# Merge gates computed first, in seven-product form and token-major, in a one-core hybrid decoder layer

## The chip, the cores and the metric

The kernel runs on one core of one Trainium2 chip. Its time is device microseconds of that core; the number given for a kernel is the median of its runs. The kernel before took 1704.99 us (three runs: 1705.82, 1704.99 and 1703.16). The rows below come from one profiled execution, whose span from the first to the last instruction is 1703.4 us.

## The reference

One decoder layer on 512 tokens of width 2048, all in float32:

```
h = rmsnorm(x) * norm_gain                      # 512 x 2048
u = h @ w_in                                    # 2048 x 12488 columns:
#   4 x 1024 fox q,k,v,z | 8 forget logits | 4 x 1024 rwkv r,k,v,z | 2 x 96 low rank | 2048 g_a | 2048 g_b
o_a = fox_attention(q, k, v, log_sigmoid(f + bias)) * silu(z_a)     # 8 heads of 128, causal softmax
o_b = (group_norm(rwkv7_scan(r, decay, k, v, kk, kk * a)) + bonus) * silu(z_b)   # 16 heads of 64
m = sigmoid(g_a) * (o_a @ w_proj_fox) + sigmoid(g_b) * (o_b @ w_proj_rwkv)       # 1024 x 2048 each
out = final_rmsnorm(x + m @ w_out)              # 2048 x 2048
```

The four thousand columns `g_a` and `g_b` are the merge gates. The RWKV inputs are shifted by a token before use (`u + (previous u - u) * mu`), and the scan is done in chunks of 64 tokens.

## The kernel before, in words

Every large product is made exact enough by splitting both operands into two parts of TensorE's float32 format, `hi + lo`, and adding three products (hi·hi, hi·lo, lo·hi). So the 128 columns of one tile of `u`, over 16 chunks of the width, are 48 matmuls with 512 moving columns each (the tokens), with the weights stationary. `load_raw` (L237) brings a piece of weights, `split_pieces` makes `whi` on ACT (L262) and `wlo` on DVE (L263); loads run five pieces ahead and splits two. `mm` (L133) and `tr` (L137) are the helpers through which nearly all TensorE instructions go.

The stages, in order:

1. Startup. `norm_rows` (L197 to L211) takes the row norms of x; `turn` (L213 to L225) turns x on TensorE, two chunks of 256 tokens at a time, and writes `hhi` on ACT (L222) and `hlo` on DVE (L225). The tile `u_wd` (low-rank inputs and forget logits) is computed behind the turning, half of the tokens after the other half.
2. `u_ad`, the second low-rank tile.
3. Sixteen units in the order rw0, rw1, fox0, rw2, fox1, ... fox5, rw7, fox6: a pair of RWKV heads (tiles k, r, z, v) or a FoX head (tiles fq, fk, fv, fz).
4. The gates `u_g` (32 tiles), three tiles ahead of the projections `p` that they gate; unit fox7 stands after the third gate tile. A projection tile is 24 matmuls.
5. The output product `o` (765 matmuls and a few more), the residual and the final norm.

The order on TensorE is the order in which the program emits it. The stream of large products is the filler; a worker for each RWKV pair (`rwkv_prep` then `rwkv_chain`) and each FoX head (`fox_head`) puts small products between. A worker yields a distance on an emission clock (the table `LAG`) and is resumed when that much other work was emitted. `until` forces workers on without filler where the stream needs something that a worker has not yet released: unit fox i waits for head i-1 to be emitted to its end, the tile k of pair i for the first step of the preparation of pair i-1. ACT, DVE and POOL are ordered by a scheduler with priorities after `start.close()`.

The scan's chain has eight chunks a pair. Each is `z` on TensorE, its copy `zt` (L689, DVE), `sa` (TensorE), two copies into `SV` (L701 on DVE, L702 on ACT), `st` (TensorE) and the new state (L710, DVE), one after the other. The inverses of the chunk triangles are 31 steps of a multiply (L478) and a sum (L620) on DVE.

Of the kernel before, what the change touches and what calls it, by code (L numbers as in the profile page):

```python
# [9 lines left out]
F32 = mybir.dt.float32  # L10
# [16 lines left out]
FW = 1024  # L27
RW0 = 4 * FW + NH             # first column of the RWKV part of w_in
# [8 lines left out]
# rows of the parameter tile, which is transposed to one column per row  # L37
# [17 lines left out]
def hybrid_layer(  # L55
# [15 lines left out]
    wpool = ctx.enter_context(tc.tile_pool(name="wpool", bufs=1))  # L71
    psm = ctx.enter_context(tc.tile_pool(name="psm", bufs=1, space=PSUM))
# [78 lines left out]
    # ---------------------------------------------------------------- loads and constants
# [4 lines left out]
    xload = ExitStack()  # L156
    xpool = xload.enter_context(tc.tile_pool(name="xpool", bufs=1))
# [4 lines left out]
    junk = xpool.tile([P, D], F32, name="junk")  # L162
# [3 lines left out]
    xts = [xpool.tile([P, D], F32, tag="xt", bufs=4, name=f"x_{tb}") for tb in range(4)]  # L166
# [24 lines left out]
    # ---------------------------------------------------------------- h = rmsnorm(x), transposed, in two parts  # L191
# [40 lines left out]
    used = [0]  # L232

    def load_raw(name, srcs, nk, M):
        raw = wpool.tile([P, nk, M], F32, tag="raw", bufs=RAWS, name=f"raw_{name}")
        for off, src in srcs:
            nc.sync.dma_start(raw[:, :, off:off + src.shape[1]], src.rearrange("(k p) m -> p k m", p=P))  # L237
        return raw

    def next_piece():  # L240
        """The two parts of the next piece of the weights. Loads run ahead of the products by
        RAWS pieces, the splits by two."""
        i = used[0]
# [8 lines left out]
    def split_pieces(n):  # L252
        while len(parts) < min(n, len(pieces)):
# [775 lines left out]
```

## Time and profile before

| | |
|---|---|
| runs | 1703.16 to 1705.82 us, median 1704.99 us |
| profiled execution, span | 1703.4 us |
| TensorE busy | 1669.6 us (98%), 8874 matmuls |
| VectorE (DVE) busy | 958.7 us (56%) |
| ScalarE (ACT) busy | 699.5 us (41%) |
| GpSimd (POOL) busy | 66.5 us (4%) |
| DMA | 170.28 MB, mean 100 GB/s |

The profiled execution is given by its span alone; the median of the runs stands 1.6 us above it. PE is TensorE, PEld its weight loads, DVE VectorE, ACT ScalarE, POOL GpSimd, SP SyncE, whose queue issues most DMAs. A busy time is the time in which an engine had an instruction running. Matmuls are pipelined, so one is listed longer (0.39 us) than the pitch from one to the next.

### The profile page before, as it was taken

To read this page: it belongs to the slowest core of one execution; us is meant where nothing else is said; L and a number is where in the kernel's file an instruction comes from. 1 tells how busy PE (TensorE), PEld (TensorE's weight loads), DVE (VectorE), ACT (ScalarE), POOL (GpSimd) and SP (SyncE) were. 2 spreads that over 40 slices of the span, in tenths; PEclk is the share of its full clock that TensorE was granted. 3 is DMA by queue.
4 is the path that set the end of the run, shared out by engine and by line. 5 is a ranking of instruction groups with operands and counts; after the bars stand their busy time and mean duration, and the time that the engine had idled before them with its cause. 6 is when DMAs were issued, how large, how long until landed. Compare 5 with 4: busy or idle time off the path is not lost.

```text
span 1703.4 us, 24080 instructions
## 1 busy us (share of the span) xinstructions
PE 1669.6 (98%) x8874; PEld 1317.2 (77%) x8874; DVE 958.7 (56%) x2005; ACT 699.5 (41%) x1391; POOL 66.5 (4%) x133
## 2 busy tenths in 40 slices
PE   6999999999999999999999999999999999999998
PEld 5778768677687786877867777888888888888886
DVE  6647568786796677866976645232224333353432
ACT  7532552554445535544454444222223222243322
POOL 3000000000000000000000000000000000001110
PEclk9999999999999999999999999999999999999999
DMA  6334234233233332333334325335334333343422
GB/s 176 77 90 110 68 88 107 61 108 92 69 97 83 86 96 81 102 79 91 82 82 111 88 76 142 98 94 148 94 99 143 98 95 98 96 141 136 136 81 99
DMA packets 287980, 170.28 MB, mean 100 GB/s; under 512 B 38790, under 2 KB 270830, under 8 KB 287222
## 3 DMA queue, kind: packets, MB, share of 16 engines
q1 hardware_dynamic: 284358, 156.13, 33.8%
q0 software_dynamic: 2064, 9.46, 1.6%
q10 hardware_dynamic: 1440, 3.15, 0.5%
q8 instruction: 69, 1.13, 0.3%
q14 instruction: 49, 0.40, 0.1%
HBM read 158.19 MB, written 10.50 MB: 99 GB/s over the span
## 4 chain that ended last, share of the span: by engine, by line
PE 94%; DVE 4%; DMA 1%; SPq 1%; ACT 1%; issue 0%; DVEq 0%; ACTq 0%
PE u_g L133 21%; PE o L133 10%; PE p L133 10%; PE u_fz L133 5%; PE u_fv L133 5%; PE u_fq L133 5%; PE u_r L133 5%; PE u_fk L133 5%; PE u_k L133 5%; PE u_v L133 5%; PE u_z L133 5%; DVE BK L478 2%; PE y L133 1%; PE fo L133 1%; PE sc L133 1%; PE sa L133 1%
## 5 line engine op out<-in xcount | busy, mean ns | idle before, releaser
L133 PE MATMUL u_g<-hhi,whi_g 128*128 128x512 f32 x512 | 200.2, 391 | 0.0
L133 PE MATMUL u_g<-hhi,wlo_g 128*128 128x512 f32 x512 | 200.1, 391 | 0.0
L133 PE MATMUL u_g<-hlo,whi_g 128*128 128x512 f32 x512 | 199.4, 390 | 0.0
L263 DVE TENSOR_TENSOR wlo_g<-raw_g,whi_g 128x512 fp32r<-128x512 f32 x128 | 88.2, 689 | 164.1 <-ACT whi_g L262 159.9
L262 ACT ACTIVATE whi_g<-raw_g 128x512 fp32r<-128x512 f32 x128 | 80.9, 632 | 226.1 <-PE u_g L133 120.1
L133 PEld LDWEIGHTS u_g<-hhi,wlo_g 128*128 128x128 f32 x512 | 96.1, 188 | 20.6
L133 PEld LDWEIGHTS u_g<-hlo,whi_g 128*128 128x128 f32 x512 | 96.1, 188 | 20.3
L133 PEld LDWEIGHTS u_g<-hhi,whi_g 128*128 128x128 f32 x512 | 96.1, 188 | 19.9
L478 DVE TENSOR_TENSOR Wt<-W,Lt 128x16 f32<-128x16 f32 (+30 forms) x248 | 101.7, 410 | 5.4
L133 PE MATMUL p<-ohi,whi_p 128*128 128x512 f32 x256 | 101.2, 395 | 0.5 <-ACT ohi L868 0.5
L263 DVE TENSOR_TENSOR wlo_p<-raw_p,whi_p 128x512 fp32r<-128x512 f32 x64 | 44.3, 692 | 102.0 <-ACT whi_p L262 102.0
L133 PE MATMUL p<-ohi,wlo_p 128*128 128x512 f32 x256 | 100.5, 392 | 0.0
L133 PE MATMUL p<-olo,whi_p 128*128 128x512 f32 x256 | 99.9, 390 | 0.5 <-DVE olo L870 0.5
L262 ACT ACTIVATE whi_p<-raw_p 128x512 fp32r<-128x512 f32 x64 | 40.4, 631 | 122.2 <-PE u_g L133 120.6
L133 PE MATMUL o<-whi_o,mhi 128*128 128x512 f32 x224 | 87.3, 390 | 0.1
L133 PE MATMUL o<-wlo_o,mhi 128*128 128x512 f32 x224 | 87.2, 389 | 0.0
L133 PE MATMUL o<-whi_o,mlo 128*128 128x512 f32 x224 | 87.1, 389 | 0.0
L263 DVE TENSOR_TENSOR wlo_o<-raw_o,whi_o 128x512 fp32r<-128x512 f32 x56 | 41.7, 755 | 63.6 <-ACT whi_o L262 63.4
L620 DVE TENSOR_REDUCE W<-Wt 128x8 f32<-128x16 f32 (+30 forms) x248 | 72.9, 294 | 5.4
L262 ACT ACTIVATE whi_o<-raw_o 128x512 fp32r<-128x512 f32 x56 | 34.7, 629 | 70.0 <-PE o L133 65.8
L133 PEld LDWEIGHTS p<-olo,whi_p 128*128 128x128 f32 x256 | 48.1, 188 | 11.9 <-DVE olo L870 1.1
L695 ACT ACTIVATE pre<-SV,E 64x64 f32<-64x64 f32 x112 | 38.5, 343 | 45.3 <-DVE SV L710 44.0
(352 smaller groups left out, 3892.1 us busy)
## 6 DMA issues: line engine op xcount, KB each, us to landing
raw_g<-in_w_in_dram SPq DMA_DIRECT2D x128, 256.0 KB
raw_o<-in_w_out_dram SPq DMA_DIRECT2D x56, 256.0 KB
raw_k<-in_w_in_dram SPq DMA_DIRECT2D x32, 256.0 KB
raw_r<-in_w_in_dram SPq DMA_DIRECT2D x32, 256.0 KB
raw_z<-in_w_in_dram SPq DMA_DIRECT2D x32, 256.0 KB
raw_v<-in_w_in_dram SPq DMA_DIRECT2D x32, 256.0 KB
raw_fq<-in_w_in_dram SPq DMA_DIRECT2D x32, 256.0 KB
raw_fk<-in_w_in_dram SPq DMA_DIRECT2D x32, 256.0 KB
```

Of the source, the lines that this page charges most:

```text
L133: PE.matmul(out, lhsT=lhsT, rhs=rhs, start=start, stop=stop, **kw)
L262: S.activation(whi, raw, AF.Copy)
L263: (G if j < 4 else V).tensor_tensor(wlo, raw, whi.bitcast(F32), ALU.subtract)
L478: eng.tensor_tensor(o, a, b, op)
L620: V.tensor_reduce(W[:, :, i], tmp[:, :, 0:i + 1], AX.X, ALU.add)
L695: S.activation(pre[hs[q]], SV[q][hs[q], c, :], AF.Copy, scale=E1[hs[q], c, CH:CH + 1])
```

## The change

Five parts, which come together:

1. The gates are computed first, right after `u_ad`, by a new function `fast`. It is the seven-product form of a two-by-two block product (Strassen's, in Winograd's ordering): the tokens are cut in two halves, the width in two halves, and the columns of a group in two blocks of 512. Four groups of 28 units of 12 matmuls make the 4096 columns. Now 128 tokens are stationary and 512 weight columns move.
2. The form needs four sums of blocks of h (`make_sums`, L260 to L273, in the second half of the startup: per step four additions or subtractions and four splits on DVE, four copies on ACT) and four sums of blocks of weights (subtractions of 128 x 1024 on DVE in `prep`). `turn` therefore keeps h in float32 and makes `hhi` with a second ACT copy.
3. The gates go through tanh and are stored in DRAM (`sg_d`, 16 stores of 512 KB on POOL's queue); the merge loads them back tile by tile.
4. The projections are token-major (merged output as stationary, weights moving, 768 matmuls as before), and the merged result is turned back by 64 TensorE transposes (`turn_merged`) before the output product.
5. `UNITS` replaces the alternation at its end by ... fox4, rw6, rw7, fox5, fox6, fox7. The constant `dynamic_dma_scratch_size=4096` is set.

```diff
-units = [("rw", 0), ("rw", 1)]
-for i in range(2, 8):
-    units += [("fox", i - 2), ("rw", i)]
-units += [("fox", 6)]
+UNITS = [("rw", 0), ("rw", 1), ("fox", 0), ("rw", 2), ("fox", 1), ("rw", 3), ("fox", 2), ("rw", 4), ("fox", 3),
+         ("rw", 5), ("fox", 4), ("rw", 6), ("rw", 7), ("fox", 5), ("fox", 6), ("fox", 7)]
...
 def turn(hf, j, dst):
...
-            S.activation(hhi[:, j + i, t], pt[:, i * 256:(i + 1) * 256], AF.Copy, scale=gcol[:, j + i:j + i + 1])
-        for i in range(2):
-            hs = hhi[:, j + i, t]
-            V.scalar_tensor_tensor(hlo[:, j + i, t], pt[:, i * 256:(i + 1) * 256], gcol[:, j + i:j + i + 1],
-                                   hs.bitcast(F32), ALU.mult, ALU.subtract)
+            S.activation(dst[:, i, :], pt[:, i * 256:(i + 1) * 256], AF.Copy, scale=gcol[:, j + i:j + i + 1])
+        S.copy(hhi[:, j:j + 2, t], dst)
+        V.tensor_tensor(hlo[:, j:j + 2, t], dst, hhi[:, j:j + 2, t].bitcast(F32), ALU.subtract)
+    def make_sums(m, a11, a12, a21, a22):
+        st = xpool.tile([P, 4, 2, 256], F32, tag="st", name=f"st_{m}")
+        s1, s2, s3, s4 = (st[:, i] for i in range(4))
+        V.tensor_tensor(s1, a21, a22, ALU.add)
+        V.tensor_tensor(s2, s1, a11, ALU.subtract)
+        V.tensor_tensor(s3, a11, a21, ALU.subtract)
+        V.tensor_tensor(s4, a12, s2, ALU.subtract)
+        for i, s in enumerate(SUMS):
+            hi, lo = (a[:, 2 * m:2 * m + 2, :] for a in sums[s])
+            S.copy(hi, st[:, i])
+            V.tensor_tensor(lo, st[:, i], hi.bitcast(F32), ALU.subtract)
...
+    def fast(name, A, rows, groups, pools, result):
+        seq = [(p, j) for j in range(4) for p in ("1", "5")] + [("6", j) for j in range(4)] + [("2", 0)]
+        seq += [("7", j) for j in range(4)]
+        seq += [("2", 1), ("4", 0), ("2", 2), ("4", 1), ("2", 3), ("4", 2), ("4", 3)] + [("3", j) for j in range(4)]
...
+        def prep(n):
...
+            elif p == "7":
+                src = raw[g, "7", j]
+                tt(V, src, Ts[j], src, ALU.subtract)
...
+            hi = wp.tile([P, 2, 512], F32R, tag="hi", bufs=3, name=f"{name}h{g}{p}{j}")
+            lo = wp.tile([P, 2, 512], F32R, tag="lo", bufs=3, name=f"{name}l{g}{p}{j}")
+            S.activation(hi, src, AF.Copy)
+            tt(V, lo, src, hi.bitcast(F32), ALU.subtract)
...
+        for n, (g, p, j) in enumerate(units):
+            load(n + 4)
+            if n + 2 < len(units):
+                prep(n + 2)
+            for kk in range(2):
+                for b in range(2):
+                    mm(ps[:, b, :], a_hi[:, k, t], w_hi[:, kk, :], ...)
+                    mm(ps[:, b, :], a_hi[:, k, t], w_lo[:, kk, :], ...)
+                    mm(ps[:, b, :], a_lo[:, k, t], w_hi[:, kk, :], ...)
...
+    for br, src in ((0, ob_d), (1, oa_d)):
+        os_ = branch(br, src)
+        for n in range(4):
+            load_gates(br, n)
+            pss = [bank(t, f"p_{br}_{n}_{t}") for t in range(4)]
+            for k in range(KB):
+                whi, wlo = next_piece()
+                for t in range(4):
+                    mm(pss[t], ohi[:, ts], whi[:, 0, :], ...)
...
+                if br == 1 and n > 0 and k == 4:
+                    yield from turn_merged(n - 1)
+            for t in range(4):
+                sg = sgs.pop((br, n, t))
...
+    yield from turn_merged(3)
```

How two places of the order change. On DVE in the second half of the startup, the turning of the last 256 tokens stood before as follows (`hlo` is the low part of h, `wlo_ad` the low part of the weights of `u_ad`):

```order
L225 SCALAR_TENSOR_TENSOR hlo<-xT_8_351,gcol,hhi 128x256 x2
L225 SCALAR_TENSOR_TENSOR hlo<-xT_10_366,gcol,hhi 128x256 x2
L225 SCALAR_TENSOR_TENSOR hlo<-xT_12_381,gcol,hhi 128x256 x2
L263 TENSOR_TENSOR wlo_ad_397<-raw_ad_186,whi_ad_396 128x384
L225 SCALAR_TENSOR_TENSOR hlo<-xT_14_400,gcol,hhi 128x256 x2
L263 TENSOR_TENSOR wlo_ad_422<-raw_ad_219,whi_ad_421 128x384
```

Now eight instructions of `make_sums` (`st` is the float32 sum, `s1l` to `s4l` its low parts) follow each two of `hlo`, four times over; the piece `wlo_ad_490`, the second of `u_ad`, comes behind the last of them:

```order
L252 TENSOR_TENSOR hlo<-hb_435,hhi 128x2x256
L266 TENSOR_TENSOR st_464<-hb_435 128x512
L267 TENSOR_TENSOR st_464<-st_464,h_108 128x512
L268 TENSOR_TENSOR st_464<-h_108,hb_435 128x512
L269 TENSOR_TENSOR st_464<-h_108,st_464 128x512
L273 TENSOR_TENSOR s1l<-st_464,s1h 128x512
L273 TENSOR_TENSOR s2l<-st_464,s2h 128x512
L273 TENSOR_TENSOR s3l<-st_464,s3h 128x512
L273 TENSOR_TENSOR s4l<-st_464,s4h 128x512
L311 TENSOR_TENSOR wlo_ad_490<-raw_ad_229,whi_ad_489 128x384
```

So the rest of `u_ad` on TensorE stands behind all of the sums. On TensorE, the chain of pair 6 ran before between the large products of fox5 (`u_fv`; `z_6` is chunk 6 of the chain, `y` its output):

```order
L133 MATMUL u_fv_8826<-hhi,whi_fv_8_8829 128x512
L133 MATMUL u_fv_8826<-hlo,whi_fv_8_8829 128x512
L133 MATMUL z_6_8917<-SV_6_7588,G_6_7759 64x64
L133 MATMUL z_6_8917<-SV_6_7589,G_6_7760 64x64
L133 MATMUL y_8542<-AR_7482,SV_6_7588 64x64
L133 MATMUL y_8542<-AR_7482,SV_6_7589 64x64
L133 MATMUL u_fv_8826<-hhi,wlo_fv_8_8830 128x512
L133 MATMUL u_fv_8826<-hhi,whi_fv_8_8829 128x512
```

Now it runs, with the preparation of pair 7 (`kn`, `lw`, `la`) and the softmax of head 5 (`fl`, `fpt`), between the last large product of fox5 and the first of fox6, 128 rows of the listing; this is a piece of it, chunk 1 of the chain:

```order
L150 MATMUL z_1_10740<-SV_6_9803,G_6_9976 64x64
L150 MATMUL z_1_10740<-SV_6_9804,G_6_9977 64x64
L150 MATMUL y_10671<-AR_9686,SV_6_9803 64x64
L150 MATMUL y_10671<-AR_9686,SV_6_9804 64x64
L150 MATMUL sa_1_10750<-zt_10743,DT_2818 64x64 x2
L154 MATMUL fpt_0_10755<-ident,pr_5_10591 128x128
L150 MATMUL fl_2_10758<-fkh_10249,fqh_10247 128x384
L150 MATMUL fl_2_10758<-fkl_10250,fqh_10247 128x384
L150 MATMUL fl_2_10758<-fkh_10249,fql_10248 128x384
L150 MATMUL st_1_10770<-SV_6_9803,BT_10569 64x64
```

No `u_` product stands between the steps of the chain there any more.

## Rows read from the trace of the kernel before

**Rows 1.** The page: the span, and TensorE's busy time (share, instructions).

```profile
span 1703.4 us, 24080 instructions
PE 1669.6 (98%) x8874; PEld 1317.2 (77%) x8874; DVE 958.7 (56%) x2005; ACT 699.5 (41%) x1391; POOL 66.5 (4%) x133
```

**Rows 2.** The chain of waits, at the stages: start us, us, what, count.

```profile
35.89 11.14 PE u_ad L133 x48
47.03 10.88 PE u_k L133 x48
...
1109.48 10.93 PE u_g L133 x48
...
1521.30 174.34 PE o L133 x765
```

**Rows 3.** TensorE in the startup: start, us, instruction, tile, operands, shapes, count.

```profile
17.51 0.60 PE L137 MATMUL xT<-ident,x 128*128 128x128 f32 x4
17.86 0.36 PE L133 MATMUL u_wd<-hhi,whi_wd 128*104 128x256 f32 x1
```

**Rows 4.** DVE in the startup and at the split of `ad`.

```profile
28.00 5.58 DVE L225 SCALAR_TENSOR_TENSOR hlo<-xT,gcol,hhi 128x256 fp32r<-128x256 f32 x14 [0.33 <-ACT hhi L222]
...
49.73 0.74 DVE L444 SCALAR_TENSOR_TENSOR ad<-u_ad,par1m,ad 96x511 f32<-96x511 f32 x1
51.15 0.69 DVE L422 TENSOR_TENSOR adl<-ad,adh 96x512 fp32r<-96x512 f32 x1 [0.69 <-ACT adh L421]
```

**Rows 5.** ACT in the startup.

```profile
27.12 5.22 ACT L222 ACTIVATE hhi<-xT,gcol 128x256 fp32r<-128x256 f32 x14 [1.36 <-PE xT L137]
...
41.79 0.62 ACT L421 CAST wdh<-wd 96x512 fp32r<-96x512 f32 x1
```

**Rows 6.** DVE: two splits of weights that follow each other.

```profile
891.56 1.28 DVE L263 TENSOR_TENSOR wlo_fv<-raw_fv,whi_fv 128x512 fp32r<-128x512 f32 x2
```

**Rows 7.** Two windows: length, busy time of each engine, granted clock, DMA share, GB/s.

```profile
575.00:692.00 117.00, 116.37 (x702) 88.81 (x702) 85.70 (x195) 57.31 (x116) 4.17 (x8) 1.00 0.36 95
1500.00:1600.00 100.00, 99.92 (x440) 82.28 (x439) 46.61 (x70) 35.70 (x66) 7.99 (x7) 1.00 0.41 142
```

**Rows 8.** DVE groups: the inversion, and two from 570 to 691 us.

```profile
L478 DVE TENSOR_TENSOR Wt<-W,Lt 128x16 f32<-128x16 f32 (+30 forms) x248 | 101.7, 410 | 5.4
L620 DVE TENSOR_REDUCE W<-Wt 128x8 f32<-128x16 f32 (+30 forms) x248 | 72.9, 294 | 5.4
...
L478 DVE TENSOR_TENSOR G<-sc,smask 128x512 f32<-128x512 f32 x6 | 4.1, 683 | 3.9 <-PE sc L133 3.9
L731 DVE RECIPROCAL ysd<-ysd 128x128 f32<-128x128 f32 x4 | 3.4, 910 | 1.6 <-ACT ysd L728 1.6
```

**Rows 9.** One chunk of a chain, on TensorE, DVE and ACT.

```profile
892.34 0.34 PE L133 MATMUL z<-SV,G 128*64 128x64 f32 x4
...
892.76 0.22 DVE L689 COPY zt<-z 128x64 f32<-128x64 f32 x1
...
893.76 0.33 PE L133 MATMUL sa<-zt,DT 64*64 64x64 f32 x4
...
894.45 0.21 ACT L702 COPY SV<-sa 64x64 f32<-64x64 f32 x1 [2.05 <-DVE SV L701]
...
896.95 0.59 DVE L710 SCALAR_TENSOR_TENSOR SV<-st,E,pre 64x64 f32<-64x64 f32 x2
```

**Rows 10.** The chain of waits where the projections begin.

```profile
1033.60 2.59 DMA oraw<-ob_d
```

**Rows 11.** Windows around a wait of TensorE, columns as in rows 7.

```profile
86.00:88.00 2.00, 0.84 (x4) 0.71 (x5) 1.97 (x4) 0.00 (x0) 0.00 (x0) 1.00 0.00 0
88.00:90.00 2.00, 2.00 (x7) 1.51 (x6) 2.00 (x4) 0.00 (x0) 0.00 (x0) 0.53 0.52 131
90.00:92.00 2.00, 2.00 (x7) 1.63 (x6) 0.86 (x2) 0.63 (x1) 0.00 (x0) 0.62 0.76 181
```

More of the change, by code (lines that the diff above doesn't have):

```diff
@@ L27 @@
 FW = 1024
+KB = 8
 RW0 = 4 * FW + NH
@@ L154, in hybrid_layer @@
     make_identity(nc, ident)
-    xload = ExitStack()
-    xpool = xload.enter_context(tc.tile_pool(name="xpool", bufs=1))
+    first = Stage()
+    now["ps"] = first.open("psm0", space=PSUM)
+    early = Stage()
+    spool = early.open("spool")
+    lora_w = Stage()
+    now["w"] = lora_w.open("wlora")
+    xload = Stage()
+    xpool = xload.open("xpool")
     start = ExitStack()
@@ L165, in hybrid_layer @@
     G.dma_start(grow, norm_gain.rearrange("o (r c) -> (o r) c", c=P))
-    xts = [xpool.tile([P, D], F32, tag="xt", bufs=4, name=f"x_{tb}") for tb in range(4)]
+    xts = [spool.tile([P, D], F32, tag=f"s4{'hl'[tb]}", name=f"x_{tb}") for tb in range(2)]
+    xts += [xpool.tile([P, D], F32, tag="xt", bufs=2, name=f"x_{tb}") for tb in (2, 3)]
     def load_x(eng, tb, hf):
@@ L232, in hybrid_layer @@
     used = [0]
+    limit = [8]
     def load_raw(name, srcs, nk, M):
-        raw = wpool.tile([P, nk, M], F32, tag="raw", bufs=RAWS, name=f"raw_{name}")
+        raw = now["w"].tile([P, nk, M], F32, tag="raw", bufs=RAWS, name=f"raw_{name}")
         for off, src in srcs:
@@ L341, in hybrid_layer @@
     MW = LORA + NH
+    lag = AHEAD // 2
     for hf in range(2):
         t = slice(256 * hf, 256 * hf + 256)
-        for j in range(0, KC + AHEAD, 2):
-            if j < KC:
-                turn(hf, j)
-            if hf == 0 and j % 4 == 0 and j < KC:
+        order = list(range(0, KC, 2)) if hf == 0 else [0, 8, 2, 10, 4, 12, 6, 14]
+        for i in range(KC // 2 + lag):
+            if i < KC // 2:
+                j = order[i]
+                if hf == 0:
+                    turn(0, j, h32[:, j:j + 2, :])
+                else:
+                    if i % 2 == 0:
+                        hb = xpool.tile([P, 4, 256], F32, tag="hb", name=f"hb_{i}")
+                    turn(1, j, hb[:, 2 * (i % 2):2 * (i % 2) + 2, :])
+            if hf == 0 and i % 2 == 0 and i < KC // 2:
                 wd_w.append(next_piece())
-                if j == 0:
+                if i == 0:
                     for tb in range(2, 4):
@@ L391, in hybrid_layer, with split, head_sums @@
                             pattern=[[1, 64]], channel_multiplier=-1)
+    bones = const.tile([P, P], F32R, name="bones")
+    lp = lora_w.open("lp")
+    ones2 = lp.tile([P, P], F32, name="ones2")
+    G.memset(ones2, 0.0)
+    G.memset(ones2[0:64, 0:64], 1.0)
+    G.memset(ones2[64:128, 64:128], 1.0)
+    S.copy(bones, ones2)
+    def split(hi, lo, a):
+        S.copy(hi, a)
+        V.tensor_tensor(lo, a, hi.bitcast(F32), ALU.subtract)
+    def head_sums(ps, hi, lo):
+        mm(ps, bones, hi, start=True, stop=False)
+        mm(ps, bones, lo, start=False, stop=True)
@@ new lines, in shift, with three @@
+    def shift(dst, ps, col, M=P):
+        mu, mu1 = par[0:M, col:col + 1], par1m[0:M, col:col + 1]
+        S.activation(dst[:, 0:1], ps[0:M, 0:1], AF.Copy, scale=mu1)
+        S.activation(dst[:, 1:T], ps[0:M, 0:T - 1], AF.Copy, scale=mu)
+        V.scalar_tensor_tensor(dst[:, 1:T], ps[0:M, 1:T], mu1, dst[:, 1:T], ALU.mult, ALU.add)
+    wds, ads = ([const.tile([LORA, T], F32R, name=f"{n}{i}") for i in "hl"] for n in ("wd", "ad"))
+    def three(ps, a, b, start=True, stop=True):
+        mm(ps, a[0], b[0], start=start, stop=False)
+        mm(ps, a[0], b[1], start=False, stop=False)
+        mm(ps, a[1], b[0], start=False, stop=stop)
@@ new lines, in hybrid_layer @@
+    wd = lp.tile([LORA, T], F32, tag="t2", name="wd")
+    shift(wd, ps_wd, R_MUW, LORA)
+    S.activation(wd, wd, AF.Tanh)
+    split(*wds, wd)
+    F0, F1 = LORA, LORA + NH
+    fx = lp.tile([P, T], F32, tag="t0", name="fx")
+    S.activation(fx[F0:F1], ps_wd[F0:F1, :], AF.Identity, bias=par[F0:F1, R_MUW:R_MUW + 1])
+    fa = lp.tile([P, T], F32, tag="a", name="fa")
+    S.activation(fa[F0:F1], fx[F0:F1], AF.Abs)
+    S.activation(fa[F0:F1], fa[F0:F1], AF.Exp, scale=-1.0)
+    S.activation(fa[F0:F1], fa[F0:F1], AF.Ln, bias=1.0)
@@ new lines, in hybrid_layer, with gate_rows @@
+    gw = early.open("gw")
+    gps = early.open("gps", space=PSUM)
+    half = [slice(0, KB), slice(KB, KC)]
+    tok = [slice(0, 256), slice(256, 512)]
+    A = {p: [a[:, half[kb], tok[th]] for a in (hhi, hlo)] for p, th, kb in (("1", 0, 0), ("2", 0, 1), ("4", 1, 1))}
+    A |= {p: sums[s] for p, s in (("5", "s1"), ("6", "s2"), ("7", "s3"), ("3", "s4"))}
+    def gate_rows(g, kb, cb, j):
+        r0 = kb * 1024 + j * 256
+        c0 = (GB0, GA0)[g // 2] + (g % 2) * 1024 + cb * 512
+        return w_in[r0:r0 + 256, c0:c0 + 512]
@@ new lines, in gate_result @@
+    def gate_result(g, th, cb, src, dst):
+        S.activation(dst, src, AF.Tanh, scale=0.5)
+        c0 = (g % 2) * 1024 + cb * 512
+        G.dma_start(sg_d[g // 2][th * 256:th * 256 + 256, c0:c0 + 512].rearrange("(b p) m -> p b m", p=P), dst)
+    for _ in fast("g", A, gate_rows, range(4), (gw, gw, gps), gate_result):
+        pass
+    early.close()
+    limit[0] = len(pieces)
+    middle = Stage()
+    ctx.callback(middle.close)
+    now["w"] = middle.open("wpool")
+    now["ps"] = middle.open("psm", space=PSUM)
@@ L824, in stage1 @@
     def stage1():
-        ps = yield from u_tile("ad")
-        ad = keep.tile([LORA, T], F32, tag="t2", name="ad")
-        shift(ad, ps, R_MUA, LORA)
-        split(*ads, ad)
         prep = chain = chain2 = None
@@ new lines, in stage1, with turn_merged @@
+        got = []
+        def turn_merged(n):
+            if not got:
+                got.extend(hpool.tile([P, KC, T], F32R, tag=t, name=nm) for t, nm in (("hi", "mhi"), ("lo", "mlo")))
+            mhi, mlo = got
+            for c in range(4):
+                k = 4 * n + c
+                pt = ps_ms(f"mT_{k}")
+                for t in range(4):
+                    tr(pt[:, t * P:(t + 1) * P], ms_[n][:, t, c * P:(c + 1) * P])
+                S.activation(mhi[:, k, :], pt, AF.Copy, scale=0.5)
+                V.scalar_tensor_tensor(mlo[:, k, :], pt, 0.5, mhi[:, k, :].bitcast(F32), ALU.mult, ALU.subtract)
+                yield
```

320 lines of the change are left out of this document (184 added, 136 removed).

## The prediction

> **What bounds the kernel now.** I read the page first. TensorE is busy for 1669.6 of 1703.4 us [rows 1]; every other engine is under 60%. The chain of waits then shows that nearly all of the rest lies ahead of `u_k`, which starts at 47.03 us, and that the large products follow one another without a hole: 48 matmuls in 10.88 to 10.93 us, whichever the tile, and 765 of the output product in 174.34 [rows 2]. So a matmul of 512 columns costs 10.93 / 48 = 0.2277 us, with the weights stationary as in `u_g` or the tokens stationary as in `o` (174.34 / 765 = 0.2279). The two windows say why: among the units and among the projections TensorE is busy for all but 0.7 us, at full clock [rows 7]. In the first window, 575 to 692 us, lie eight tiles, 384 large matmuls or 87.4 us; the other 29 us are small products of a pair and a head, and while these run, DVE has 85.7 us of work of its own and hides all of it behind the large ones. Time can come from fewer matmuls; it is lost wherever TensorE has to stand still for DVE or ACT.
>
> **What the change removes.** The gates take 4 x 28 x 12 = 1344 matmuls instead of 32 x 48 = 1536. At the same pitch, 192 x 0.2277 = 43.7 us less.
>
> **What it adds to TensorE.** 64 transposes of 128 x 128. Four of them take 17.86 - 17.51 = 0.35 us [rows 3], so 64 x 0.0875 = +5.6 us. The projections keep 768 matmuls, the output product stays.
>
> **Startup: +22.** In the first half each step gets one more ACT copy of 512 elements, 0.62 us alone [rows 5], about 0.52 in a row; ACT is the engine waited for there: 8 x 0.52 = 4.2. In the second half DVE now does ten instructions of 512 elements a step where it did four of 256. Two of 512 take 1.28 us, so 0.64 each [rows 6]; with about 0.3 us for ACT's copies that the splits wait for, a step is 6.7 us and four are 26.8. Before, fourteen of 256 elements took 5.58 us, 0.40 each [rows 4]. `hlo` began at 28.0; now 32.2, and the last sum ends at 59.0. The second weight piece of `u_ad` is split behind it, at 59.6, and 36 matmuls (8.2 us) and the start-up of the clock bring the end of `u_ad` to about 69, where it was 47.03. The bounds: +10 if the sums of one step were hidden behind ACT's turning of the next (ACT's fourteen take 5.22 [rows 5]), +28 if each split stands alone at 0.69 plus a hand-off.
>
> **From `u_ad` to the first gate: +5.5.** The shift and the split of `ad` now stand ahead of the gates' first splits in DVE's order: before, `adl` ended at 51.84, 4.8 us behind the end of `u_ad` [rows 2, 4], hidden behind `u_k`. Half a microsecond of that was other work of DVE, and the first split of 1024 elements (1.2, below) follows, with nothing beside it. Bounds 1 and 7.
>
> **Inside the gates: +3.** A unit is 12 x 0.2277 = 2.73 us. The trace has no DVE instruction of 1024 elements. By the pair [rows 6] one lies between 0.64 us (a second half for nothing) and 1.28; I take 1.2, near the upper end, as 256 elements take 0.40 and 512 take 0.64, which is 0.24 more for each 256. A group has 24 to 28 splits, 16 subtractions and five additions at its end, 49 in all: 59 us of its 76.5. Where a unit needs two, 2.4 of 2.73. The preparation is two units ahead, so DVE fits, barely. A group reads 24 x 512 KB, 165 GB/s, and writes 2 MB; 181 GB/s passed in a window at a DMA share of 0.76 [rows 11]. Bounds: 0, and +57 (the rival below).
> [...]
>
> **From the gates to the units: +4.5.** The raw weights of `u_k` of pair 0 take memory that the gates held, so their load cannot start ahead of the last gate matmuls; before, it ran behind `u_ad`. 2.59 us to land, as 256 KB do [rows 10], 0.62 and 0.69 to split [rows 4, 5], and 0.6 for issue. Bounds 2 and 7.
>
> **The tail of the units.** With rw6 and rw7 side by side and fox5, fox6 and fox7 in a row, the stream has to force workers on.
> - Tile k of pair 7 waits for the preparation of pair 6: +4 (bounds 0 and 10).
> - Between fox5 and fox6 stand 128 rows of small products: all eight chunks of chain 6, the preparation of pair 7, the head 5. TensorE has about 20 us of work in them (two thirds of the 29 above). DVE has, for a pair and a head, 85.7 - 32 splits x 0.69 = 63.7 us, less 31 x (0.410 + 0.294) = 21.8 of the inversion, less about 9 for the masks of the scores and the group norm [rows 7, 8], which lie outside: 33. Nothing large covers it, and DVE in turn waits for TensorE and ACT, some 10 us more: 43, so +22. Bounds: +8 (DVE busy from the first moment on work that it could begin earlier) and +40 (chain, preparation and head one after another).
> - Between fox6 and fox7 stand head 6 and six chunks of chain 7. A bare chunk is z, zt, sa, SV on DVE and on ACT, st, the new state: 0.34 + 0.22 + 0.33 + 0.22 + 0.21 + 0.34 + 0.59 [rows 9]; what is not shown there costs what its like does. The sum is 2.25, and some 0.1 for each of seven hand-offs: 2.9. Six are 17.4, the rest of head and inverse about 10, against 14.5 of TensorE's own work: +12.5. Bounds +4 and +22.
>
> **Projections and output: +8.5.** In the second branch each block of columns reuses its PSUM banks, and DVE clears a bank with a product and a sum: 3 x 0.9. The fourth group of transposes waits for one of three banks: 3 x 0.85. At the end the last transposes wait for DVE's last sum, and the output for their split: 3.5 more than the 0.7 us before. Bounds 3 and 15.
>
> **The clock.** Where TensorE had waited (86 to 88 us), the granted clock stood at 0.53 and 0.62 in the next two windows [rows 11], which is its lower level of 1.2 GHz for most of them: (0.47 + 0.38) x 2 = 1.7 us lost; after longer holes more. For four or five such holes I put +10 (bounds 4 and 25, as small products in the gaps run at the low level too).
> The Trainium skill ("TensorE: Matmul & The Clock Gate", section "Terms") takes the penalty as the throttled time times one minus the ratio, and the throttled state as the default; this trace agrees in these two windows, and no stretch of before shows a hole of 40 us. It speaks against a change that opens such holes; what it would make of them is the third rival.
>
> **The sum.** -43.7 + 5.6 + 22 + 5.5 + 3 + 4.5 + 4 + 22 + 12.5 + 8.5 + 10 = +53.9. Against the span of 1703.4 that is 1757; the median of the runs stood 1.6 above the span, so I say 1758.
>
> **Rivals.**
> - *DVE and ACT are always ahead.* The scheduler lets them run each small step as soon as its operands stand, and in TensorE's order the steps lie later than their operands need: TensorE then never waits behind the startup. For it: in the units before, waits are almost nil [rows 7]. Against: that cover was the large products, which the two gaps do not have. It decides between the last product of fox5 and the first of fox6: TensorE would be busy for nearly all of about 20 us. Price: 1705 - 43.7 + 5.6 + 22, with 5.5, 3 and 8.5 for handover, gates and projections: 1706, not slower; with the startup at its lower bound 1694. Chance 0.08.
> - *The gates run at DVE's pace.* If subtraction, ACT's copy and split come one after another and do not overlap over units (1.2 + 1.2 + 1.2, about 3.7 us), the 16 units with two DVE steps take 3.7 instead of 2.73: 16 x 4 x 0.97 = 62, less the 3 above: about 1817. For it: DVE is 77% busy by my count, with three buffers for each split. Against: the two units of lead. Chance 0.12.
> - *The gaps run at the low clock throughout.* Then the small products in both gaps, 34.5 us of TensorE's work at the full clock, take twice that, and if chain and softmax wait for them one after another, the 34.5 come on top, in place of the 10 above: 1782. For it: 0.53 and 0.62 after a wait of about 1 us [rows 11]. Against: while TensorE works slower, DVE gets on, and its 33 us are the longer part. Chance 0.10.
> - *The change does not do what it says.* The order shows 1344 gate matmuls and 64 transposes; under 0.01.
>
> **The numbers.** My case has 0.69, with its own range from 1726 to 1796 by its bounds (not all at one end together). It holds the third rival; the first lies outside below and the second above, so it has the time 8 times in 10. A measurement of this kernel tells 0.2% (3.4 us) from no change. Faster by more: 0.06, from the first rival; within: 0.03; slower: 0.91.
>
> **What would show it.** `u_ad` ends near 69 us; the gates last 306 us or little more from there; TensorE is idle for about 20 us between fox5 and fox6, with `zt`, `SV` and softmax rows of DVE as what it waited for, and for about 12 between fox6 and fox7; the output product starts about 54 us later than 1521.3. It would be wrong if the gates' end came over 30 us later than 69 + 5.5 + 306, or if those holes were under 5 us.

## The result, and the profile after

The changed kernel takes 1781.0 us (four runs, 1779.13 to 1781.72), the kernel before 1705.07 beside it: 1.0446 times as long, 95% interval 1.0431 to 1.0461. The forecast was 1758, from 1726 to 1796, and slower at 0.91. The sign and most of the parts held; the loss of 76 us is 22 more than the 54 of the sum, and its terms for the gates and for the tail of the units were too small.

The page of the changed kernel, span, busy times and the granted clock in 40 slices of 44 us:

```profile
span 1777.3 us, 23857 instructions
PE 1683.9 (95%) x8746; PEld 1322.9 (74%) x8746; DVE 1122.6 (63%) x2089; ACT 763.4 (43%) x1396; POOL 78.0 (4%) x149
PEclk8799999999999999999999998996879999999999
```

Where TensorE was busy for all but 34 us [rows 1], 93 us are open now, and the clock is down at the beginning and in four slices between 1066 and 1333 us. The stages stand in the chain of waits and in the first and last starts of the tiles (start us, us, what, count; for the tile the shortest, median and longest matmul in ns, then first and last start):

```profile
L150 PE MATMUL u_ad<-hhi,wlo_ad x16: 392/397/595, 58.6 to 69.5; 128*96 128x512 f32 x16
```

```profile
76.38 4.23 PE gX L150 x11
...
382.87 10.68 PE gZ L150 x48
393.56 3.01 DMA raw_k<-in_w_in_dram
397.33 12.59 PE u_k L150 x48
...
1594.55 15.48 PE o L150 x67
```

The first row of the output product itself, which the chain enters a little later:

```profile
1594.20 0.78 PE L150 MATMUL o<-whi_o,mhi 128*128 128x512 f32 x1
```

These rows answer to [rows 2], and with them every stage can be set against the forecast. In the table 1474.3 us is the way from `u_k` to `o` in the kernel before (1521.30 - 47.03), and 349.7 its 1536 gate matmuls at 0.2277 us:

| part | forecast | measured | from |
|---|---|---|---|
| `u_ad` ends (47.03 before) | +22 | +22.8 | 69.5 and the last matmul, 69.8 |
| to the first gates | +5.5 | +6.6 | 76.4 - 69.8 |
| gates, 1344 matmuls at their pitch are 306.0 | -43.7 + 3 | -43.7 + 11.2 | 393.55 - 76.38 = 317.2, against 32 x 10.93 |
| gates to `u_k` | +4.5 | +3.8 | 397.33 - 393.55 |
| transposes of the merge | +5.6 | +5.6 | 64, as counted |
| units, projections, up to `o`, with the clock | +57 | +66.7 | (1594.2 - 397.3) - (1474.3 - 349.7) - 5.6 |
| `o` and the end | 0 | +1.0 | 1777.3 - 1594.2 = 183.1 against 1703.4 - 1521.3 = 182.1 |

The parts make +74.0; the spans differ by 73.9. The tail is where the engines show best. The last large products of fox5 and fox6 and the first of fox6 and fox7 (TensorE's own rows):

```profile
1205.53 0.39 PE L150 MATMUL u_fz<-hhi,wlo_fz 128*128 128x512 f32 x1
...
1258.74 0.50 PE L150 MATMUL u_fq<-hhi,whi_fq 128*128 128x512 f32 x1
...
1304.74 0.39 PE L150 MATMUL u_fz<-hhi,wlo_fz 128*128 128x512 f32 x1
1339.86 0.50 PE L150 MATMUL u_fq<-hhi,whi_fq 128*128 128x512 f32 x1
```

The first of these ends fox5, and the second is the next large product, of fox6: a gap of 53 us. The other two rows bound the gap ahead of fox7, 35 us. The windows of the first one, columns as in [rows 7]:

```profile
1210.00:1220.00 10.00, 6.26 (x52) 4.02 (x54) 3.98 (x11) 7.21 (x15) 0.00 (x0) 0.64 0.34 90
1220.00:1230.00 10.00, 8.89 (x59) 6.29 (x59) 7.22 (x17) 5.05 (x13) 0.61 (x1) 0.50 0.00 0
1230.00:1240.00 10.00, 5.45 (x32) 3.77 (x32) 8.41 (x21) 6.46 (x19) 1.27 (x1) 0.50 0.01 2
1240.00:1250.00 10.00, 7.41 (x52) 5.24 (x54) 6.49 (x16) 2.20 (x7) 0.00 (x0) 0.50 0.00 0
1250.00:1260.00 10.00, 9.73 (x59) 6.30 (x59) 3.02 (x8) 1.98 (x8) 0.28 (x1) 0.65 0.01 2
```

TensorE is not idle for long at a stretch, yet it gets little done: 32 to 59 small matmuls in 10 us where the projections have 44 large ones, mostly at half the clock, and no engine is full. Over both gaps, from the end of one large product to the start of the next:

```profile
1205.92:1258.74 52.82, 39.72 (x291) 27.35 (x288) 32.02 (x79) 26.09 (x67) 1.88 (x2) 0.58 0.08 21
1305.13:1339.86 34.73, 27.01 (x215) 19.27 (x213) 15.24 (x51) 15.26 (x46) 0.00 (x0) 0.61 0.17 41
```

TensorE was idle for 13.1 us of the first gap and 7.7 of the second. That picture allows two readings, a low clock that lengthens the gaps and a chain of hand-offs that sets their length; the last experiment below was to choose between them.

### The profile page after: what moved, and what is told of

Same layout as the page of the kernel before. It is cut to its first block, busy times and chain, and to the rows that moved or that the text cites. A ratio compares the mean times of both kernels' runs of the same rounds, so it can differ in the third digit from the quotient of the medians.

```text
span 1777.3 us, 23857 instructions
## 1 busy us (share of the span) xinstructions
PE 1683.9 (95%) x8746; PEld 1322.9 (74%) x8746; DVE 1122.6 (63%) x2089; ACT 763.4 (43%) x1396; POOL 78.0 (4%) x149
## 4 chain that ended last, share of the span: by engine, by line
PE 78%; DVE 10%; DMA 6%; ACT 4%; issue 2%; SPq 1%; DVEq 0%; ACTq 0%
PE o L150 10%; PE p L150 8%; PE gY L150 6%; PE u_fq L150 5%; PE u_k L150 5%; PE u_r L150 5%; PE u_fk L150 5%; PE u_v L150 5%; PE u_z L150 5%; PE u_fv L150 4%; DMA gb<-in_w_in_dram 4%; PE u_fz L150 4%; PE gX L150 3%; DVE BK L503 1%; PE y L150 1%
## 5 line engine op out<-in xcount | busy, mean ns | idle before, releaser
L150 PE MATMUL p<-whi_p,ohi 128*128 128x512 f32 x256 | 102.6, 401 | 3.3 <-DVE fz L1003 2.5
L150 PE MATMUL p<-wlo_p,ohi 128*128 128x512 f32 x256 | 102.0, 398 | 0.2 <-DVE wlo_p L311 0.2
L150 PE MATMUL p<-whi_p,olo 128*128 128x512 f32 x256 | 101.8, 398 | 0.0
L557 ACT ACTIVATE gh<-gb 128x1024 fp32r<-128x1024 f32 x64 | 67.9, 1061 | 78.7 <-PE gY L150 51.5
L503 DVE TENSOR_TENSOR gl<-gb,gh 128x1024 fp32r<-128x1024 f32 x64 | 77.8, 1220 | 29.1 <-ACT gh L557 27.8
L150 PE MATMUL o<-whi_o,mhi 128*128 128x512 f32 x224 | 87.5, 391 | 0.0
L150 PE MATMUL o<-wlo_o,mhi 128*128 128x512 f32 x224 | 87.3, 390 | 0.0
L150 PE MATMUL o<-whi_o,mlo 128*128 128x512 f32 x224 | 87.1, 389 | 0.0
L557 ACT ACTIVATE gh<-gT 128x1024 fp32r<-128x1024 f32 x48 | 50.9, 1060 | 70.1 <-PE gX L150 27.6
L503 DVE TENSOR_TENSOR gl<-gT,gh 128x1024 fp32r<-128x1024 f32 x48 | 58.3, 1221 | 15.4 <-ACT gh L557 15.3
L150 PEld LDWEIGHTS p<-whi_p,ohi 128*128 128x128 f32 x256 | 48.4, 189 | 16.5 <-DVE fz L1003 3.0
L150 PEld LDWEIGHTS p<-whi_p,olo 128*128 128x128 f32 x256 | 48.5, 189 | 11.6
L150 PEld LDWEIGHTS p<-wlo_p,ohi 128*128 128x128 f32 x256 | 48.5, 189 | 11.6 <-DVE wlo_p L311 0.5
L150 PE MATMUL u_k<-hhi,whi_k 128*128 128x512 f32 x128 | 53.4, 417 | 3.6 <-ACT whi_k L310 3.6
L150 PE MATMUL gX<-gl,hhi 128*128 128x512 f32 x128 | 51.4, 401 | 5.6 <-DVE gl L503 5.6
```

Source lines behind the costliest of these rows:

```text
L150: PE.matmul(out, lhsT=lhsT, rhs=rhs, start=start, stop=stop, **kw)
L503: eng.tensor_tensor(o, a, b, op)
L557: S.activation(hi, src, AF.Copy)
```

## The experiments

All were run beside the kernel before (1703.6 to 1705.1 us); "changed" is the 1781.0 above.

**Without the sums of h.** The call of `make_sums` is left out, and the products take blocks of h.

```diff
-                make_sums(m, h32[:, 2 * m:2 * m + 2, :], ...)
...
-    A |= {p: sums[s] for p, s in (("5", "s1"), ("6", "s2"), ("7", "s3"), ("3", "s4"))}
+    A |= {p: A[q] for p, q in (("5", "1"), ("6", "2"), ("7", "4"), ("3", "1"))}
```

> The changed kernel without the sums of blocks of h: the eight DVE and four ACT instructions of each step of the startup are left out, and the seven-product form takes blocks of h in their place (the gates are then not the reference's; the count of matmuls, loads and weight subtractions is unchanged). Theory (DVE's sums set the startup's end): u_ad ends near 53 us instead of 69.8, the rest is unchanged, 1764 us (1759 to 1769). Rival (turning, ACT's second copy and the low clock set it anyway): u_ad ends above 63 us, 1775 or more.

1766.1 us, 14.9 less. `u_ad` ends at 59.9:

```profile
L150 PE MATMUL u_ad<-hhi,wlo_ad x16: 389/394/401, 49.2 to 59.7; 128*96 128x512 f32 x16
```

The time is in the theory's range, the end of `u_ad` in neither's: the sums cost 9.9 us of the startup, not 17, and 12.9 stay without them. ACT's second copies, which the sums had hidden, now set the pace: DVE waits for them, and from one step (two of `hlo`) to the next it is 3.70 us.

```profile
37.25 0.69 DVE L252 TENSOR_TENSOR hlo<-hb,hhi 128x512 fp32r<-128x512 f32 x1 [1.62 <-ACT hhi L251]
...
40.95 0.69 DVE L252 TENSOR_TENSOR hlo<-hb,hhi 128x512 fp32r<-128x512 f32 x1 [1.61 <-ACT hhi L251]
```

The rest of the gain is at the handovers, where the first gates stand 1.9 us closer to `u_ad`, and the load of `raw_k` no longer waits for the last gate products: `u_k` follows `gZ` without a hole (384.66 behind 373.78 + 10.88 in the chain). The gate stage itself was 2.7 us longer.

**The old turning too.** The same, with `hhi` and `hlo` written as before, straight from PSUM.

```diff
-            S.activation(dst[:, i, :], pt[:, ...], AF.Copy, scale=gcol[...])
-        S.copy(hhi[:, j:j + 2, t], dst)
-        V.tensor_tensor(hlo[:, j:j + 2, t], dst, hhi[:, j:j + 2, t].bitcast(F32), ALU.subtract)
+            S.activation(hhi[:, j + i, t], pt[:, ...], AF.Copy, scale=gcol[...])
+        V.scalar_tensor_tensor(hlo[:, j + i, t], pt[:, ...], gcol[...], hs.bitcast(F32), ALU.mult, ALU.subtract)
```

> The run without sums once more, and with the turning of the kernel before in place of the new one (high part of h straight from PSUM on ACT, low part on DVE, no float32 copy of h; the gates are not the reference's). The run without sums ended u_ad at 59.9 us, 12.9 later than before. Theory (the second ACT copy of each step does that, in both halves): u_ad ends near 47 to 48 us, and the time is 1766 - 12 = 1754 us (1751 to 1757). Rival (the order of the blocks and the pools of the new startup do it): u_ad ends above 55 us, 1761 or more.

1752.7 us, 13.4 less again, and `u_ad` ends as in the kernel before:

```profile
L150 PE MATMUL u_ad<-hhi,wlo_ad x16: 389/394/400, 36.7 to 47.1; 128*96 128x512 f32 x16
```

Taken away in this order, the startup's 22.8 us are 9.9 of the sums and 12.9 of the new turning, which is the second ACT copy and the split that now waits for it. In the changed kernel the second half begins, a DVE step runs and the last sum ends so:

```profile
33.69 0.69 DVE L252 TENSOR_TENSOR hlo<-hb,hhi 128x512 fp32r<-128x512 f32 x1 [1.13 <-ACT hhi L251]
...
42.38 0.68 DVE L266 TENSOR_TENSOR st<-hb 128x512 f32<-128x512 f32 x1
...
46.72 0.69 DVE L273 TENSOR_TENSOR s4l<-st,s4h 128x512 fp32r<-128x512 f32 x1
47.32 0.69 DVE L252 TENSOR_TENSOR hlo<-hb,hhi 128x512 fp32r<-128x512 f32 x1
...
49.07 0.68 DVE L266 TENSOR_TENSOR st<-hb 128x512 f32<-128x512 f32 x1
...
60.51 0.69 DVE L273 TENSOR_TENSOR s4l<-st,s4h 128x512 fp32r<-128x512 f32 x1
```

From one `st` of a step to the next it is 49.07 - 42.38 = 6.69, as forecast. A step that DVE fills for 6.7 us hides the extra ACT copies of the second half; take the sums away and they come to light. So the two numbers belong to this order of taking away, and are not shares of one path.

**Plain gates at the same place.** Three-product form, 128 tokens stationary, no sums and no weight subtractions; each piece of 256 weight rows is used for all four token blocks.

```diff
-    for _ in fast("g", A, gate_rows, range(4), (gw, gw, gps), gate_result):
-        pass
+    plain("g", gate_rows, range(4), (gw, gw, gps), gate_result)
...
+            for kk in range(2):
+                for b in range(4):
+                    mm(o, hhi[:, k, t], w_hi[:, kk, :], ...)
+                    mm(o, hhi[:, k, t], w_lo[:, kk, :], ...)
+                    mm(o, hlo[:, k, t], w_hi[:, kk, :], ...)
```

> The gates in plain three-product form at the same place, token-major as in the changed kernel: 1536 matmuls instead of 1344, 64 loads of 512 KB instead of 96, no sums of h and no weight subtractions; all else as changed. Theory (the form saves its 43.7 us less what DVE and the loads hold it up, about 11, and its sums cost 17 in the startup): 1764 + 43.7 - 10 = about 1798, so the form itself is worth only some 17 us net where it stands, and the place of the gates costs the rest. Rival (the holes in the gate stage come with any gates at this place, loads of 512 KB in a row): 1808 or more. Rival (the form is worth nothing net): 1781 or less.

1797.1 us, as the theory had it. In the changed kernel's place the seven-product form is worth 16 us net of the 43.7 that it saves in matmuls. Its gate stage has no holes: 349.8 us from the first `gl` product to `u_k`, where 1536 matmuls at their pitch are 349.7. The other side of the same number: gates in the old form, merely moved to the front and turned token-major with the rest of the change, the new turning of h among it, cost 92 us (1797.1 against 1704.8).

**Without the weight subtractions.** The raw blocks of the weights are split in place of the differences.

```diff
-                tt(V, src, raw[g, "6", j], src, ALU.subtract)
+                src = raw[g, "6", j]
```

(and so for the products 5, 7 and 4.)

> The changed kernel without the 64 subtractions of weight blocks (128 x 1024 on DVE, 1.22 us each; the raw blocks go into the split in their place, so the gates are not the reference's); loads, matmuls and stores unchanged. Theory (in the holes of gate groups 1 to 3 DVE waits for a load in its order and then, with two instructions a unit, cannot catch up): the gate stage takes 307 us instead of 317, 1771 us (1769 to 1774). Rival (eight and more loads of 512 KB in a row are the limit): the holes stay, 1778 to 1782.

1769.8 us, 11.2 less. The holes in the gate stage are gone; its last group ends at 383.9 instead of 393.6. A window of the first hole in the changed kernel and the whole of it, then the same stretch of this run, and DVE in the hole of the changed kernel:

```profile
160.00:170.00 10.00, 8.76 (x38) 6.62 (x37) 6.53 (x7) 4.25 (x5) 0.08 (x1) 1.00 0.89 269
140.00:183.00 43.00, 40.42 (x173) 31.67 (x172) 31.64 (x28) 18.64 (x18) 1.43 (x2) 1.00 0.76 232
```

```profile
140.00:184.00 44.00, 44.00 (x195) 36.41 (x194) 21.94 (x19) 21.36 (x21) 2.15 (x3) 1.00 0.78 228
```

```profile
176.90 1.23 DVE L503 TENSOR_TENSOR gb<-gT,gb 128x1024 f32<-128x1024 f32 x1 [1.54 <-DMA gb<-in_w_in_dram]
178.04 1.22 DVE L503 TENSOR_TENSOR gl<-gT,gh 128x1024 fp32r<-128x1024 f32 x1
179.18 1.22 DVE L503 TENSOR_TENSOR gb<-gT,gb 128x1024 f32<-128x1024 f32 x1
180.31 1.22 DVE L503 TENSOR_TENSOR gT<-gb,gT 128x1024 f32<-128x1024 f32 x1
```

DVE waits for a load at its head, 1.54 us, and behind it runs one instruction after the other with 1.14 us from start to start; where a unit of 2.73 us has two of them, it hardly catches up, and TensorE loses some 3 us in each of groups 1 to 3. Without the subtractions the data come at the same rate (228 GB/s against 232), TensorE has no hole, and DVE waits for no load between 100 and 390 us, where in the changed kernel it waits for 34.4 us in all. So DVE's work makes the holes, not the rate of the loads. How it does so is not separated: by its own time, or by giving back late the buffers that the loads wait for (the chain of waits through the first hole goes by turns over loads and DVE; two more buffers, in the next run, closed no hole).

An instruction of 1024 elements takes 1.22 us; the forecast had 1.2. By the Trainium skill ("VectorE: DVE Perf Modes", section "The TRN2 errata"), whose formula for a float32 `tensor_tensor` of N elements is (N + 151) / 0.96 ns, an estimate is 1.224 us; the trace agrees within 5 ns.

**Deeper loads.** Six buffers instead of four, loads two units earlier.

```diff
-                t = wp.tile([P, 2, 512], F32, tag="bs", bufs=4, ...)
+                t = wp.tile([P, 2, 512], F32, tag="bs", bufs=6, ...)
...
-            load(n + 4)
+            load(n + 6)
```

> The changed kernel with six buffers instead of four for the raw gate weights, and loads issued two units earlier. Theory (the holes at the start of gate groups 1 to 3 come from a load that is issued when a buffer comes free and lands 4 to 6 us later): about 3 us less for each of three groups, 1772 us (1769 to 1775). Rival (the eight loads in a row ask for more than the DMA engines give, or DVE is the limit): 1779 to 1783.

1779.7 us (1777.4 to 1781.1), no change that can be told. My theory falls that issuing the loads earlier would close the holes. Its rival names two causes; the run above picks DVE's work.

**The order of units alone, in the kernel before.**

```diff
-    for i in range(2, 8):
+    for i in range(2, 7):
         units += [("fox", i - 2), ("rw", i)]
-    units += [("fox", 6)]
+    units += [("rw", 7), ("fox", 5), ("fox", 6)]
```

> The kernel before with the new order of units alone: rw6, rw7, fox5, fox6 at the end in place of rw6, fox5, rw7, fox6; the gates stay behind, three of them ahead of fox7. In TensorE's order the same 128 rows of small products then stand between fox5 and fox6 as in the changed kernel. Theory (that gap took 53 us for 20 us of work, whoever follows, because no large product covers it; and the second pair beside the first costs some 8 more): 1705 + 33 + 8 = 1746 us (1735 to 1752). Rival (the gap is long in the changed kernel because of what the gates left behind, not because of the order): 1705 to 1715.

1739.0 us, 1.0208 times the time (1.0193 to 1.0224), 35 us. The gap stands there as in the changed kernel, 55 us from fox5's last product to fox6's first:

```profile
853.70 0.39 PE L133 MATMUL u_fz<-hhi,wlo_fz 128*128 128x512 f32 x1
...
908.84 0.51 PE L133 MATMUL u_fq<-hhi,whi_fq 128*128 128x512 f32 x1
```

So the order of the units costs 35 us by itself, about half of the whole loss, with the gates untouched.

**The old order of units, in the changed kernel.** `... rw6, fox5, rw7, fox6, fox7`.

```diff
-         ("rw", 5), ("fox", 4), ("rw", 6), ("rw", 7), ("fox", 5), ("fox", 6), ("fox", 7)]
+         ("rw", 5), ("fox", 4), ("rw", 6), ("fox", 5), ("rw", 7), ("fox", 6), ("fox", 7)]
```

> The changed kernel with the old order of units at the end: rw6, fox5, rw7, fox6, fox7. In TensorE's order the gap of 128 rows between fox5 and fox6 is gone; 39 rows of head 6 stand between fox6 and fox7. Theory (the order costs most of the tail): -33 for the first gap, -8 for the pair, -5 of the second gap, and the end of chain 7 comes later by some 10: 1745 us (1738 to 1755). Rival (with the gates gone the tail has too little cover in any order, so the waits only move): 1770 or more.

1769.2 us: 11.8 less, where theory had 36 and the rival at most 11. The first gap is gone. The one ahead of fox7 is as long as before (36 us, from the last product of fox6 at 1270.2 to 1306.4), now with a new wait in it (what TensorE waited for between 1080 and 1420 us; total, times, longest):

```profile
PE gp L150 <- DVE A L827: 14.8, 2, 14.6
PE fpt L154 <- ACT pr L959: 8.9, 2, 4.8
PE p L150 <- DVE olo L1063: 5.6, 1, 5.6
PE p L150 <- ACT ohi L1061: 4.1, 1, 4.1
```

`gp` of pair 7 needs the inverse, 31 steps on DVE, and nothing large is left that could run beside it; then the projections wait for the last chain. Nearly what the rival said: without the gates there is too little cover for chain 7 and heads 6 and 7 in either order.

**Cover put back.** The old order, the last 1024 gate columns as eight plain tiles behind fox6 (three) and fox7 (five), each turned by four transposes and stored.

```diff
+UNITS += [("g", i) for i in range(3)] + [("fox", 7)] + [("g", i) for i in range(3, 8)]
...
-    for _ in fast("g", A, gate_rows, range(4), (gw, gw, gps), gate_result):
+    for _ in fast("g", A, gate_rows, range(3), (gw, gw, gps), gate_result):
```

> The changed kernel with the old order of units, and the last quarter of the gates (1024 columns) not in the seven-product form at the start but as eight plain tiles at the end: three between fox6 and fox7, five behind fox7; each is turned by four transposes and stored like the others. That costs 87.5 - 76.5 - 3.3 (holes of a group) + 2.8 (transposes) = about +10 us of large work. Theory (only cover is missing in the tail, which lost about 50 us): 1781 - 50 + 10 = 1741 us (1733 to 1750). Rival (chain 7 and head 6 end last whatever lies beside them): 1765 or more. Against the run with the old order alone, the theory says within 8 us; a filler that covers nothing would be 10 us worse.

1741.4 us (1.022 times the kernel before, 1.0204 to 1.0235). 39.6 us come back, although some 10 us of large work are added; against the old order alone it is 27.8. The theory's number was 1741. Where in the changed kernel the clock is at a half, this run's windows have TensorE at work at the full clock, beside large products (either reading of the gaps allows that):

```profile
1240.00:1250.00 10.00, 10.00 (x64) 6.83 (x63) 3.70 (x10) 3.00 (x7) 0.00 (x0) 1.00 0.21 52
1250.00:1260.00 10.00, 10.00 (x67) 6.85 (x66) 3.60 (x10) 3.46 (x9) 0.00 (x0) 1.00 0.32 80
```

**Is it the clock?** Idle large matmuls, into a bank that nobody reads, at each forced step in the two gaps: four, two or one.

```diff
+            for _ in range(4):
+                mm(ps, bones, hhi[:, 0, :])
             yield "wait"
```

> The changed kernel with about 200 idle large matmuls (512 columns, 0.2277 us each at full clock, into a bank that nobody reads) between the forced steps ahead of fox6 and of fox7: about 108 (24.6 us) and 92 (20.9 us). Theory (in these gaps TensorE's small products run at the low clock, which is granted because the large products are missing, and that is why the gaps take 53 and 28 us): the clock stays at 1.0 there, the added work takes the time that the low clock cost, 1770 to 1786 us. Rival (DVE, ACT and the hand-offs between them set the length and the clock does not matter, but the added work fits into the waits): 1778 to 1784 with TensorE busy and gaps as long as before. Second rival (TensorE's own chain sets the length; the added work comes on top): 1805 to 1826 us.

> Two idle matmuls after each forced step: 102 in all, 23 us of work. Theory (the low clock lengthens the gaps): the clock is at 1.0 there and the time is below 1781, 1768 to 1778. Rival (waits for DVE and ACT set the length): 1781 to 1790 with the clock at 1.0.

> As the run with idle matmuls in the two gaps, but one after each forced step instead of four: 51 in all, 11.6 us of work at full clock. It is to tell apart what that run left open: four a step (46.5 us) kept the clock at 1.0 and cost 16 us. Theory (the low clock lengthens the gaps): where one a step is enough to hold the clock up for most of the gaps, the time falls below the changed kernel's 1781, to 1765 to 1775. Rival (waits for DVE and ACT set the length; idle matmuls only fill them or come on top): 1781 to 1793, whatever the clock. If the clock stays near 0.5, the run tells nothing and the next one decides.

Four a step: 1796.9 us, between what the theory and the second rival said, so that run alone settled nothing. Two a step: 1786.7 (1783.6 to 1790.3; it had 114 idle matmuls, not the 102 expected). One: 1787.6, scattered from 1779.5 to 1792.3. No median came below 1781. The two gaps with four, then with two, then with one (without any they are the windows of the section above):

```profile
1206.78:1264.47 57.69, 52.77 (x405) 37.41 (x404) 32.75 (x78) 25.49 (x65) 1.89 (x2) 0.94 0.06 15
1310.51:1354.48 43.97, 42.01 (x311) 29.02 (x310) 16.31 (x53) 15.55 (x46) 0.00 (x0) 0.96 0.14 33
...
1206.90:1265.84 58.94, 49.76 (x365) 32.81 (x364) 32.99 (x80) 26.30 (x67) 2.65 (x3) 0.83 0.07 18
1311.13:1347.45 36.32, 34.12 (x272) 22.56 (x272) 14.77 (x51) 15.53 (x46) 0.00 (x0) 0.91 0.16 39
...
1209.74:1266.79 57.05, 44.71 (x319) 29.08 (x318) 33.27 (x79) 26.30 (x67) 2.16 (x2) 0.70 0.07 20
1313.16:1346.20 33.04, 27.97 (x237) 18.44 (x236) 15.34 (x51) 15.58 (x46) 0.00 (x0) 0.90 0.18 42
```

At a clock of 0.94 the first gap is no shorter. But that does not clear the clock, because the idle matmuls stand ahead of the small ones in TensorE's order and fill the gap themselves. With four a step TensorE is busy for 52.8 of 57.7 us, and the chain of waits goes over them from step to step:

```profile
1222.17 1.13 PE dummy L150 x4
1223.30 0.27 PE z L150 x4
1223.57 0.26 PE y L150 x4
1223.83 1.13 PE dummy L150 x4
```

In all 28.7 us of that chain are idle matmuls (17.2 with two a step, 11.9 with one). What it has besides them in the first gap is 29.0, 41.7 and 45.1 us, against 52.8 without any. So what the clock gives back and what the idle work takes cannot be told apart here. With one a step the second gap even got shorter, 33.0 us at a clock of 0.90 against 34.7 at 0.61, although 22 idle matmuls stand in it; in four other runs with this order of units it is 34.0 to 35.0.

How much the low clock can be worth is an estimate from the chains. In the changed kernel the chain of the first gap is 26.9 us of TensorE, 13.4 of DVE, 10.0 of ACT and 2.5 in which the engine waited for nothing that the profile shows; in the second gap TensorE has 21.4 of 34.7. Three of TensorE's pieces in the first (`lw` with `la`, `sc` and `fo`) took 2.93, 2.06 and 3.53 us there, and 1.41, 1.09 and 2.16 at the full clock in the run with four, 0.55 as long. By that, 12 and 10 us of the two chains are the low clock's. These are upper estimates, since waits for DVE and ACT come to light where TensorE is faster. What is shown: the first gap comes with the order of the units (the run with the order alone) and the time goes where large products are put beside the small work (cover put back). How the length of the gaps divides between the low clock and the hand-offs stays open.

## Why the prediction was right, and where its terms were off

- *Bound by TensorE, fewer matmuls, 43.7 us.* Right: where the weight subtractions are left out, the stage has no holes and takes 307.2 us (76.65 to 383.89), against 306.0 by the sum, and the plain gates keep the pitch too.
- *Startup +22.* Right in size (22.8) and in its path. `hlo` of the second half began at 33.69 (32.2 in the forecast), a DVE step took 6.69 (6.7), the last sum ended at 61.2 (59.0). It was my expectation for the run without sums that failed, 17 us for what gave 9.9: the second ACT copy is made in the second half as well, and there it was hidden only as long as DVE had the sums.
- *To the gates +5.5, to the units +4.5.* Held: 6.6 and 3.8. The second one's cause was given too widely. The load waited because its memory was read by the last gate products, and it goes without a wait where these read no sums; in the run with the plain gates `u_k` follows at once too.
- *Inside the gates +3.* Mis-sized: 11.2. The term was built from DVE's mean, 59 of 76.5 us. DVE waits for loads for 34.4 us between 100 and 390 us, and with up to two instructions in each unit it has hardly slack to catch up. The rival that gave the gates DVE's pace had the place and the engine, but at about +60 not the size.
- *The tail.* The first gap was to be 43 us and was 53, the second 27 and was 35. Both were worked out as DVE's time plus some 10 us of hand-offs, with TensorE's work, 20 and 14.5 us at the full clock, hidden beside it. DVE's time in the first gap was right: 32.0 us, 33 in the forecast. TensorE's was not: it was busy for 39.7 and 27.0 us at clocks of 0.58 and 0.61, and it is on the chain of waits for 26.9 us of the first gap. So the sign that I had named, TensorE idle for about 20 and 12 us and waiting for DVE, came only in part: it was idle for 13.1 and 7.7, and its longest wait in the first gap was for ACT (`PE bn L150 <- ACT rhi L455: 3.9, 1, 3.9`). The order alone, tried in the kernel before, costs 35 us where the terms for that gap and for pair 7 made 26.
- *Projections and output +8.5.* Right in the sum (8.2), in part by luck: 2.5 us of waiting where they begin were not in the forecast, the clearing of the banks cost 0.7 instead of 2.7, the transposes 4.7 and what stands behind them 1.0 where the forecast had about 6.
- *The clock +10.* Open. The estimate from the chains allows up to 22 us in the two gaps. The third rival, gaps at the low clock throughout, gave 1782 us and came nearest to the time, and what it said of TensorE came: 66.7 us of work in the two gaps, where twice its 34.5 is 69. But it let all of the 34.5 come on top, which is more than that estimate allows, and no run shows the share. A number that fits is not yet a cause.
- *The rival that ends on the other side*, DVE and ACT always ahead, was to be decided between fox5 and fox6: a stretch of about 20 us with TensorE busy for nearly all of it. It was 53 us, with TensorE idle for 13.

Not separated are the low clock and the hand-offs in the gaps, the hand-off to the gates (6.6) and the exact share of pair 7's preparation in the tail. A version that beats the kernel before was not found: with the cover put back 38 us are missing. The startup, the way to the gates and the transposes add 35.0 by the table above, more than the 32.8 (144 matmuls) that the three groups left in the seven-product form save.

## What to carry to other kernels

A product with fewer multiplications pays for its additions on the engines that make them, and at the place where they stand: 43.7 us of TensorE became 16 net, since the sums sat in a startup with nothing beside them and the subtractions filled DVE. Large products are also what hides serial work; before moving them, list what runs beside them now, and ask what will stand there instead. Where a second engine prepares the operands and is busy for three quarters of the stage, count its instructions unit by unit and not on the mean, because what it loses in one wait is then hardly made up for. And where idle work is put in to raise a clock, read from the chain of waits whether it has become the limit itself, before its time is taken for an answer.

## What the runs showed of the hardware

- A DVE instruction on 128 x 1024 float32 operands takes 1.22 us, 1.14 from start to start, against 0.69 and about 0.60 for 512: less than twice as long.
- Among small products the granted clock stayed at 0.50 from 1214 to 1256 us on end, although TensorE counted as busy for 21.8 of the 30 us from 1220 to 1250. Idle large matmuls between the steps, four, two or one, brought the mean over that gap from 0.58 to 0.94, 0.83 and 0.70.
- Loads of 512 KB with rows of 2 KB, with the stores of the gates beside them, moved 269 GB/s at a DMA share of 0.89 between 160 and 170 us, and their rate was not the limit: without the weight subtractions the same loads left no hole.
